# A hybrid decoder layer: eight of its 22 weight units as seven block products, interleaved with the rest

## The chip, the cores and the metric
One core of one Trainium2 chip runs the kernel. The metric is the device time of one execution in microseconds (us); lower is better. The profile is one execution recorded by the hardware profiler. In it PE is TensorE's matmuls, PEld its weight loads, DVE is VectorE, ACT is ScalarE, POOL is GpSimd, and SP is the engine that issues most transfers.

## The reference: what is computed
One decoder layer over 256 tokens `x` and 256 memory tokens `mem`, both 2048 wide, in fp32. `proj = x @ w_in` yields fifteen pieces of 1024 columns: q, k, v and a gate z for block attention; u, v and z for a spatial gating unit; q and z for attention into memory; and three branch gates of 2048 columns.

```python
y_a = _moba_attention(q_a, k_a, v_a) * silu(z_a)          # 8 heads of 128, causal over the 256 tokens
y_g = _spatial_gating(u_g, v_g, w_s, b_s, ln_v_g, ln_v_b) * silu(z_g)
y_c = _memory_attention(q_c, mem @ w_mem_k, mem @ w_mem_v) * silu(z_c)   # 4 heads of 256
gates = sigmoid(g_logit).reshape(b, s, 3, d)
merged = (gates[:, :, 0] * (y_a @ w_branch_attn)
          + gates[:, :, 1] * (y_g @ w_branch_sgu)
          + gates[:, :, 2] * (y_c @ w_branch_mem))
x = _layer_norm(DN_ALPHA * x + merged @ w_out, ln_g, ln_b)
```

The weights make 22 units of 2,097,152 elements (2048x1024, or half of a 1024x2048 pair): 15 in `w_in`, two for the memory's keys and values, three branch projections, two in `w_out`.

## The kernel before, in words
Nearly all arithmetic on TensorE is a product of a weight unit with 256 token columns. To keep fp32 accuracy at the speed of the float32r type, every operand is split: `split` (L41 to L43) writes a high part `hi`, the value rounded to float32r, on ScalarE, and a low part `lo = v - hi` on VectorE. A product then takes three passes: high by high, high by low, low by high.

Weights come in 176 chunks of 1 MB (8 a unit), in the order in which they are used. `load_chunk` issues the load of a chunk on SP's queue (L71) into one of three `raw` buffers; `split_chunk` splits its two halves (128x1024 each) into rings of four `hi` and four `lo` tiles; `feed` loads three chunks ahead and splits one ahead.

There are two forms of product. Channel-major (`channels_out`, L196, with `channels_mm`, L192): the weights are the stationary operand and the moving one holds the high and low parts of 256 tokens, so each block of 128x128 weights takes a matmul of 512 columns (L193) and one of 256 (L194); the result has channels on the partitions, and `joined` (L206 to L209) adds its two halves. Token-major (`tokens_out`, L163, and the output projection, L553): the tokens are stationary and the moving operand is 512 weight columns, so three matmuls of 512 columns serve a block of 128 inputs, 128 tokens and 512 channels. `vg`, `va`, `mv` and the output projection are token-major; the other 17 units, with all gates and branch projections, are channel-major.

The stages follow one another: `vg`, `u`, `zg` with the spatial mixing; `gated_branch(1)`; `va`, `za`, `q` and `k` with block attention; `gated_branch(0)`; `mv`, `mk`, `zc`, `qc` with memory attention; `gated_branch(2)`; output projection, residual and layer norm. Attention works on split parts too (`mm3`, L186: three matmuls for each product). `pending` and `tick` spread the stages of a head over the tiles of the next projection. `gated_branch` (L335 to L360) computes gate tiles with a sigmoid, then branch tiles, multiplies them and sums the three branches in `macc`; the last one splits the sum into `mhl`, the operand of the output projection. The order of each engine's instructions is not the program's: a planner, `TileContext(nc, schedule_with_timeline_sim=True)`, lays them out by the times it expects, and assigns each tile a free buffer of its tag.

## Time and profile before

| what | value |
|---|---|
| median of 3 runs | 1031.0 us (1030.88 to 1031.11) |
| span of the profiled execution | 1029.1 us |
| median minus span | 1.9 us |
| TensorE busy | 1016.3 us, 99% |
| VectorE busy | 628.8 us, 61% |
| ScalarE busy | 519.9 us, 51% |
| moved | 198.06 MB, 192 GB/s over the span |

The profile gives the span, from the first to the last instruction; the profiled execution's own time is not recorded apart from it, so the 1.9 us that the median lies above the span stand for what lies around it. Matmuls are pipelined and the profile models their ends, so the duration of one matmul is longer than the distance to the next; prices are best read from a whole stretch divided by its count. The granted clock was 1.00 wherever TensorE had work.

### The profile page before, as it was taken

What the parts mean: (1) busy time and instruction counts of PE and PEld (TensorE: products, weight loads), DVE (VectorE), ACT (ScalarE), POOL (GpSimd) and SP (SyncE); (2) the same over time, 40 slices, a digit from 0 to 9 for tenths busy, and PEclk for the clock granted to TensorE, in tenths of its full rate; (3) what the DMA queues carried; (4) which work ended last, traced back from release to release, by engine and by line L of the source; (5) the groups of instructions that cost most, each with busy time, mean ns of one, the idle gap of its engine ahead of it and who ended that gap; (6) DMA issues with size and microseconds to landing.
All of it is one profiled execution on the core that took longest, in us unless ns stands there. A gap on an engine that the chain in (4) does not pass through costs nothing.

```text
span 1029.1 us, 14329 instructions
## 1 busy us (share of the span) xinstructions
PE 1016.3 (99%) x5672; PEld 883.2 (86%) x5672; DVE 628.8 (61%) x888; ACT 519.9 (51%) x781; POOL 2.7 (0%) x10
## 2 busy tenths in 40 slices
PE   9999999999999999999999999999999999999995
PEld 7888888888888888888888888888888888888885
DVE  5584665556545456776866664556566576666756
ACT  6465554444445445557644543446455655555430
POOL 0000000000000000000000000000000000000000
PEclk9999999999999999999999999999999999999998
DMA  9855455545555544444655555545553555557722
GB/s 344 326 179 204 164 179 190 203 171 199 197 178 199 187 181 168 165 166 167 246 183 187 204 180 189 203 171 198 179 184 130 204 210 199 179 189 278 256 80 82
DMA packets 31300, 198.06 MB, mean 192 GB/s; under 512 B 3457, under 2 KB 4225, under 8 KB 8705
## 3 DMA queue, kind: packets, MB, share of 16 engines
q1 hardware_dynamic: 30672, 192.95, 52.3%
q10 hardware_dynamic: 560, 4.19, 1.1%
q8 instruction: 44, 0.72, 0.3%
q14 instruction: 24, 0.19, 0.0%
HBM read 195.04 MB, written 2.10 MB: 192 GB/s over the span
## 4 chain that ended last, share of the span: by engine, by line
PE 98%; DVE 1%; DMA 0%; DVEq 0%; ACT 0%; issue 0%; SPq 0%
PE g L193 17%; PE g L194 9%; PE b L193 9%; PE b L194 4%; PE za L193 3%; PE zc L193 3%; PE mk L193 3%; PE qc L193 3%; PE q L193 3%; PE k L193 3%; PE u L193 3%; PE zg L193 3%; PE o L558 3%; PE o L556 3%; PE o L557 3%; PE vg L178 2%
## 5 line engine op out<-in xcount | busy, mean ns | idle before, releaser
L43 DVE TENSOR_TENSOR lo<-raw,hi 128x1024 fp32r<-128x1024 f32 (+1 forms) x350 | 426.3, 1218 | 345.6 <-ACT hi L42 343.9
L42 ACT ACTIVATE hi<-raw 128x1024 fp32r<-128x1024 f32 (+1 forms) x350 | 369.5, 1056 | 432.3 <-PE g L193 116.7
L193 PE MATMUL g<-xhl,hi 128*128 128x512 f32 x768 | 270.3, 395 | 0.0
L194 PE MATMUL g<-xhl,lo 128*128 128x256 f32 x768 | 214.9, 280 | 0.0
L193 PEld LDWEIGHTS g<-xhl,hi 128*128 128x128 f32 x768 | 144.0, 188 | 33.4
L194 PEld LDWEIGHTS g<-xhl,lo 128*128 128x128 f32 x768 | 144.9, 189 | 0.2
L193 PE MATMUL b<-yhl,hi 128*128 128x512 f32 x384 | 135.6, 395 | 0.0
L194 PE MATMUL b<-yhl,lo 128*128 128x256 f32 x384 | 107.2, 280 | 0.0
L193 PEld LDWEIGHTS b<-yhl,hi 128*128 128x128 f32 x384 | 71.9, 188 | 16.4
L194 PEld LDWEIGHTS b<-yhl,lo 128*128 128x128 f32 x384 | 72.4, 189 | 0.2
L556 PE MATMUL o<-hi,mhl 128*128 128x512 f32 (+1 forms) x128 | 46.4, 363 | 0.0
L557 PE MATMUL o<-lo,mhl 128*128 128x512 f32 (+1 forms) x128 | 46.4, 362 | 0.0
L558 PE MATMUL o<-hi,mhl 128*128 128x512 f32 (+1 forms) x128 | 46.4, 362 | 0.0
L193 PE MATMUL q<-xhl,hi 128*128 128x512 f32 x128 | 45.8, 398 | 0.0
L193 PE MATMUL k<-xhl,hi 128*128 128x512 f32 x128 | 45.7, 396 | 0.0
L193 PE MATMUL qc<-xhl,hi 128*128 128x512 f32 x128 | 45.7, 399 | 0.0
L193 PE MATMUL zg<-xhl,hi 128*128 128x512 f32 x128 | 45.3, 397 | 0.0
L193 PE MATMUL zc<-xhl,hi 128*128 128x512 f32 x128 | 45.3, 399 | 0.0
L193 PE MATMUL za<-xhl,hi 128*128 128x512 f32 x128 | 45.3, 399 | 0.0
L193 PE MATMUL mk<-memhl,hi 128*128 128x512 f32 x128 | 45.3, 399 | 0.0
L193 PE MATMUL u<-xhl,hi 128*128 128x512 f32 x128 | 44.8, 396 | 0.0
L194 PE MATMUL q<-xhl,lo 128*128 128x256 f32 x128 | 36.4, 284 | 0.0
(217 smaller groups left out, 1572.8 us busy)
## 6 DMA issues: line engine op xcount, KB each, us to landing
raw<-in_w_gate_dram SPq DMA_DIRECT2D x48, 1024.0 KB, 4.8
raw<-in_w_br_dram SPq DMA_DIRECT2D x24, 1024.0 KB, 4.8
raw<-in_w_qk_dram SPq DMA_DIRECT2D x16, 1024.0 KB, 4.8
raw<-in_w_o_dram SPq DMA_DIRECT2D x16, 1024.0 KB, 4.7
raw<-in_w_ug_dram SPq DMA_DIRECT2D x8, 1024.0 KB, 5.1
raw<-in_w_zg_dram SPq DMA_DIRECT2D x8, 1024.0 KB, 4.8
raw<-in_w_va_dram SPq DMA_DIRECT2D x8, 1024.0 KB, 4.8
raw<-in_w_za_dram SPq DMA_DIRECT2D x8, 1024.0 KB, 4.8
```

The source lines that it names most:

```text
L42: nc.scalar.activation(hi, v, AF.Copy)
L43: nc.vector.tensor_tensor(lo, v, hi.bitcast(F32), op=ALU.subtract)
L178: nc.tensor.matmul(ps[t][n], xh, hi[:, n * 512:(n + 1) * 512], start=(k == 0), stop=False)
L193: nc.tensor.matmul(ps, hi, xhl[:, k, :], start=first, stop=False)
L194: nc.tensor.matmul(ps[:, S:2 * S], lo, xhl[:, k, 0:S], start=False, stop=last)
L556: nc.tensor.matmul(ps[:, 0:n], mh, hi, start=first, stop=False)
L557: nc.tensor.matmul(ps[:, 0:n], mh, lo, start=False, stop=False)
L558: nc.tensor.matmul(ps[:, 0:n], ml, hi, start=False, stop=last)
```

## The change
Eight units (the six gate units, `va` and `vg`) leave the chunk stream. Each is a product of a 256x2048 matrix with a 2048x1024 one, cut into two by two blocks. Seven block products in the Winograd order (`PRODUCTS`) replace the eight of the plain form. The sums of blocks of x are formed once (`sums`), split and stored in DRAM, and read again for each unit (`xsf`). The differences of weight blocks are formed on VectorE in place (`sub` in `s_prep`) for three of the seven products and once more for a fourth, and every product's weight operand is split, 2048 columns at a time. The products accumulate in four PSUM banks, with copies (`keep`) of intermediate sums on ScalarE and final additions (`result`) on VectorE. A unit is 14 steps: half of each of the seven products, 12 matmuls of 512 columns.

The memory's values and keys come first, on their own. After that `classic`, the stream of all other units, runs together with `s_stream`: a loop takes a step of `classic` (half a chunk: 2.8 us or so of matmuls) and, in proportion, steps of the product stream, so that 112 product steps go with the `classic` steps 3 to 146. The order of the branches is now memory, block attention, spatial gating. The branch projections become token-major (`gated_branch`), as their gates are; the gates' logits are stored in DRAM by the product stream and loaded again, `mk`, `mv`, `va`, the z and u tiles and the running sum of branches likewise, and the merged result is transposed on TensorE (`merged`). Attention multiplies unsplit fp32 operands, one matmul for each product. The raw chunk buffers go from three to two, the rings of `hi` and `lo` from four to three; all transfers are issued on SP's queue.

```diff
+    def new_acc(name):
+        return psum.tile([P, 512], F32, tag="acc", name=name, bufs=3)
+    def new_sps(name):
+        return psum.tile([P, 512], F32, tag="sps", name=name, bufs=3)
+    def new_aux(name, shape):
+        return psum.tile(list(shape), F32, tag="aux", name=name, bufs=2)
...
+    late, pending = [], []
+    def step(run):
+        old = late[:]
+        del late[:]
+        run()
+        for fn in old:
+            fn()
...
+        t = wts.tile([P, 2, 1024], F32, tag="raw", name=f"raw{i}", bufs=2)
+        raw[i] = t
...
+    def c_half(ahead=2):
+        while len(ready) < ahead + 1 and ptr["half"] < 2 * len(chunks):
+            prep_half()
+        return ready.pop(0)
...
-    def gated_branch(b):
-        sg = {}
-        for m in range(8):
-            for n in gates_before(m):
-                ps = channels_out(xhl, f"g{b}_{n}")
-                g = work.tile([P, S], F32, tag="gate", name=f"sg{b}_{n}", bufs=4)
-                joined(g, ps)
-                nc.scalar.activation(g, g, AF.Sigmoid)
-                sg[n] = g
-                tick()
-            halves = next_chunk()
-            for i in range(2):
-                n = 2 * m + i
-                hi, lo = halves[i]
-                ps = new_acc(f"b{b}_{n}")
-                for k in range(8):
-                    channels_mm(ps, yhl[b], k, hi[:, k * P:(k + 1) * P], lo[:, k * P:(k + 1) * P], k == 0, k == 7)
-                br = work.tile([P, S], F32, tag="t256", name=f"br{b}_{n}", bufs=4)
-                joined(br, ps)
-                if order[b] == 0:
-                    nc.vector.tensor_tensor(macc[:, n], br, sg[n], op=ALU.mult)
-                else:
-                    nc.vector.tensor_tensor(br, br, sg[n], op=ALU.mult)
-                    nc.vector.tensor_tensor(macc[:, n], macc[:, n], br, op=ALU.add)
-                if order[b] == 2:
-                    split(mhl[0][:, n, 0:S], mhl[0][:, n, S:2 * S], macc[:, n])
...
+                s1, s2, s3, s4 = (F[g][:, i] for i in range(4))
+                nc.vector.tensor_tensor(s1, a21, a22, op=ALU.add)
+                nc.vector.tensor_tensor(s2, s1, a11, op=ALU.subtract)
+                nc.vector.tensor_tensor(s3, a11, a21, op=ALU.subtract)
+                nc.vector.tensor_tensor(s4, a12, s2, op=ALU.subtract)
...
+                t = wts.tile([P, 4, 2 * P], F32R, tag="xsf", name=f"xw{g}{i}", bufs=3)
+                split(t[:, :, 0:P], t[:, :, P:2 * P], F[g][:, i])
+                late.append(lambda: nc.sync.dma_start(xf_d[i + 1, g], t.bitcast(F32)))
...
+    UNITS = 8
+    PRODUCTS = ("M1", "M5", "M6", "M3", "M7", "M4", "M2")
+    FORM = {"M5": 1, "M6": 2, "M3": 4, "M7": 3}
+    rt, shl, xsf, sp = {}, {}, {}, {}
...
+    def s_load(u, blk, h):
+        if u >= UNITS:
             return
...
+        tag, bufs = ("rA", 2) if blk == 0 else ("rB", 4)
+        t = wts.tile([P, 2048], F32, tag=tag, name=f"b{blk}_{u}_{h}", bufs=bufs)
+        nc.sync.dma_start(t, w_st[u, blk, h])
+        rt[u, blk, h] = t
...
+    def s_prep(s):
+        u, r = divmod(s, 14)
+        if u >= UNITS:
+            return
+        p, h = divmod(r, 2)
+        p = PRODUCTS[p]
+        if p in FORM:
+            t = wts.tile([P, 4, 2 * P], F32R, tag="xsf", name=f"xf{s}", bufs=3)
+            nc.sync.dma_start(t.bitcast(F32), xf_d[FORM[p], h])
+            xsf[s] = t
+        b = lambda blk: rt[u, blk, h]
+        sub = lambda o, x, y: nc.vector.tensor_tensor(o, x, y, op=ALU.subtract)
+        src = {"M1": B11, "M5": B11, "M6": B11, "M4": B11, "M3": B22, "M7": B12, "M2": B21}[p]
+        if p == "M5":
+            sub(b(B11), b(B12), b(B11))
+        elif p == "M6":
+            sub(b(B11), b(B22), b(B11))
+        elif p == "M4":
+            sub(b(B11), b(B21), b(B11))
+        hi = wts.tile([P, 2048], F32R, tag="shl", name=f"sh{s}", bufs=4)
+        lo = wts.tile([P, 2048], F32R, tag="shl", name=f"sl{s}", bufs=4)
+        split(hi, lo, b(src))
+        shl[s] = (hi, lo)
+        if p == "M3":
+            sub(b(B12), b(B22), b(B12))
+            s_load(u, B21, h)
+        elif p == "M7":
+            s_load(u + 1, B12, h)
+        elif p == "M4":
+            s_load(u + 1, B11, h)
+        elif p == "M2":
+            s_load(u + 1, B22, h)
...
+        def keep(name, ps):
+            kept[name] = snap(name)
+            nc.scalar.activation(kept[name], ps, AF.Copy)
+        def result(u, t, n, ps, name):
+            r = kept[name]
+            nc.vector.tensor_tensor(r, ps, r, op=ALU.add)
+            finish(u, t, n, r)
+        def evacuate(u, p):
+            if p == "M1":
+                keep(f"k1_{u}", bank["b"])
+            elif p == "M5":
+                keep(f"k5_{u}", bank["d"])
+            elif p == "M6":
+                keep(f"k6_{u}", bank["b"])
+            elif p == "M3":
+                result(u, 0, 1, bank["d"], f"k6_{u}")
+            elif p == "M7":
+                keep(f"k7_{u}", bank["b"])
+                result(u, 1, 1, bank["b"], f"k5_{u}")
+            elif p == "M4":
+                result(u, 1, 0, bank["c"], f"k7_{u}")
+            else:
+                result(u, 0, 0, bank["a"], f"k1_{u}")
+        BANK = {"M1": "b", "M6": "b", "M7": "b", "M5": "d", "M3": "d", "M4": "c", "M2": "a"}
+        for s in range(14 * UNITS):
+            u, r = divmod(s, 14)
+            p, h = divmod(r, 2)
+            p = PRODUCTS[p]
+            if h == 0 and p in ("M1", "M5", "M4", "M2"):
+                bank[BANK[p]] = new_sps(f"s{p}_{u}")
+            ps = bank[BANK[p]]
+            hi, lo = shl.pop(s)
+            for kk in range(4):
+                k = 4 * h + kk
+                if p in FORM:
+                    ah, al = xsf[s][:, kk, 0:P], xsf[s][:, kk, P:2 * P]
+                else:
+                    k += 0 if p == "M1" else 8
+                    t = P if p == "M4" else 0
+                    ah, al = xhl[:, k, t:t + P], xhl[:, k, S + t:S + t + P]
+                c = slice(kk * 512, (kk + 1) * 512)
+                first = h == 0 and kk == 0 and p in ("M1", "M5", "M4", "M2")
+                last = h == 1 and kk == 3
+                nc.tensor.matmul(ps, ah, hi[:, c], start=first, stop=False, skip_group_check=True)
+                nc.tensor.matmul(ps, ah, lo[:, c], start=False, stop=False, skip_group_check=True)
+                nc.tensor.matmul(ps, al, hi[:, c], start=False, stop=last, skip_group_check=True)
+            xsf.pop(s, None)
+            s_prep(s + 2)
+            if h == 1:
+                late.append(lambda u=u, p=p: evacuate(u, p))
+            yield
...
+    for _ in run(mem_values()):
+        pass
+    for i, _ in enumerate(run(mem_keys())):
+        if i >= 1 and x_work:
+            x_work.pop(0)()
+    while x_work:
+        x_work.pop(0)()
+        step(lambda: None)
+    for blk in (B11, B12, B22):
+        for h in range(2):
+            s_load(0, blk, h)
+    s_prep(0)
+    s_prep(1)
...
+            ps = new_aux(f"ms{h}", (P, 2, S))
+            for t in range(2):
+                for kk in range(2):
+                    nc.tensor.matmul(ps[:, t], q[kk][:, t * P:(t + 1) * P], st["k"][:, kk],
+                                     start=(t == 0 and kk == 0), stop=(t == 1 and kk == 1), skip_group_check=True)
...
+            nc.tensor.matmul(ps[:, P:384], q[:, P:S], k, start=False, stop=True, skip_group_check=True)
...
+            nc.tensor.matmul(ps, st["v"][:, 0], st["pt"][:, 0:S], start=True, stop=False, skip_group_check=True)
+            nc.tensor.matmul(ps[:, P:S], st["v"][:, 1], st["pt"][:, S:384], start=False, stop=True,
+                             skip_group_check=True)
...
+    def gated_branch(b, order):
+        for n in range(4):
+            ps = [new_acc(f"b{b}_{n}{t}") for t in range(2)]
+            g, prev = {}, {}
+            for t in range(2):
+                g[t] = w2(f"sg{b}{t}{n}")
+                nc.sync.dma_start(g[t], gl_d[b, t, n])
+                nc.scalar.activation(g[t], g[t], AF.Sigmoid)
+            for half in range(4):
+                hi, lo = c_half()
+                for kk in range(2):
+                    k = 2 * half + kk
+                    c = slice(kk * 512, (kk + 1) * 512)
+                    for t in range(2):
+                        yh, yl = (yhl[b][:, k, o + t * P:o + (t + 1) * P] for o in (0, S))
+                        nc.tensor.matmul(ps[t], yh, hi[:, c], start=(k == 0), stop=False)
+                        nc.tensor.matmul(ps[t], yh, lo[:, c], start=False, stop=False)
+                        nc.tensor.matmul(ps[t], yl, hi[:, c], start=False, stop=(k == 7))
+                if half == 3:
+                    late.append(lambda n=n, ps=ps, g=g: gated(b, order, n, ps, g))
+                yield
+    def gated(b, order, n, ps, g):
+        for t in range(2):
+            if order:
+                prev = w2(f"mp{b}{t}{n}")
+                nc.sync.dma_start(prev, mc_d[order - 1, t, n])
+            nc.vector.tensor_tensor(g[t], ps[t], g[t], op=ALU.mult)
+            if order:
+                nc.vector.tensor_tensor(g[t], g[t], prev, op=ALU.add)
+            if order < 2:
+                store(mc_d[order, t, n], g[t])
+            else:
+                pending.append([lambda t=t: merged(n, t, g[t])])
         tick()
...
+    def merged(n, t, m):
+        if t == 0:
+            mhl.append(wts.tile([P, 4, 2 * S], F32R, tag="shl", name=f"mhl{n}", bufs=4))
+        ps = new_aux(f"mT{n}{t}", (P, 4, P))
+        for i in range(4):
+            nc.tensor.transpose(ps[:, i], m[:, i * P:(i + 1) * P], ident)
+        split(mhl[n][:, :, t * P:(t + 1) * P], mhl[n][:, :, S + t * P:S + (t + 1) * P], ps)
...
+    def s_finish(u, t, n, r):
+        if u in GATES:
+            b, half = GATES[u]
+            store(gl_d[b, t, 2 * half + n], r)
+        elif u == 2:
+            store(va_d[t, n], r)
+        else:
+            if vg[0] is None:
+                vg[0] = big.tile([P, 2, W], F32, tag="vg", name="vg")
+            nc.scalar.activation(vg[0][:, t, n * 512:(n + 1) * 512], r, AF.Copy)
+            if (t, n) == (0, 0):
+                pending.append(sgu_norm())
+    GATES = {0: (2, 0), 1: (2, 1), 3: (0, 0), 4: (0, 1), 6: (1, 0), 7: (1, 1)}
+    def classic():
+        yield from gate_tiles("zc", AF.Silu, szc_d)
+        new_y(2)
+        yield from mem_attention()
+        yield from drain()
+        yield from gated_branch(2, 0)
+        yield from gate_tiles("za", AF.Silu, sza_d)
+        new_y(0)
+        yield from block_attention()
+        yield from drain()
+        yield from gated_branch(0, 1)
+        yield from gate_tiles("ug", AF.Gelu_apprx_tanh, gu_d)
+        new_y(1)
+        yield from gating()
+        yield from drain()
+        yield from gated_branch(1, 2)
+    def drain():
+        yield None
+        while pending:
+            tick()
+            yield None
+    C_STEPS, S_STEPS = 160, 14 * UNITS
+    LEAD, TAIL = 2, 14
+    cs, ss = classic(), s_stream(s_finish)
+    done_c = done_s = 0
+    for _ in run(cs):
+        done_c += 1
+        while done_s < S_STEPS and done_s * (C_STEPS - LEAD - TAIL) < (done_c - LEAD) * S_STEPS:
+            step(lambda: next(ss))
+            done_s += 1
...
+    def blocks(w):
+        b = w.reshape(2, 2, 4, P, 2, 512).transpose(0, 4, 1, 3, 2, 5).reshape(2, 2, 2, P, D)
+        return np.stack([b[0, 0], b[0, 1], b[1, 1], b[1, 0]])
```

## Rows read from the trace of the kernel before
**Rows 1.** The page: busy time of each engine; the chain that ended last, by engine.
```profile
PE 1016.3 (99%) x5672; PEld 883.2 (86%) x5672; DVE 628.8 (61%) x888; ACT 519.9 (51%) x781; POOL 2.7 (0%) x10
...
PE 98%; DVE 1%; DMA 0%; DVEq 0%; ACT 0%; issue 0%; SPq 0%
```
**Rows 2.** Windows by stage: stretch, length, busy us (instructions) by engine, clock, DMA share, GB/s.
```profile
50.90:96.20 45.30, 45.30 (x262) 39.49 (x261) 31.73 (x43) 25.89 (x38) 0.00 (x0) 1.00 0.53 189
...
143.50:277.00 133.50, 133.50 (x774) 117.73 (x773) 78.24 (x102) 66.47 (x100) 0.00 (x0) 1.00 0.52 187
277.00:320.50 43.50, 43.50 (x194) 35.99 (x193) 20.77 (x21) 18.11 (x19) 0.00 (x0) 1.00 0.54 191
320.50:365.80 45.30, 45.30 (x258) 39.24 (x257) 24.30 (x27) 23.48 (x34) 0.00 (x0) 1.00 0.53 189
...
929.30:994.50 65.20, 65.20 (x289) 54.01 (x288) 41.24 (x49) 30.18 (x31) 0.00 (x0) 1.00 0.64 232
994.50:1018.00 23.50, 23.44 (x194) 23.17 (x192) 12.95 (x32) 2.55 (x3) 0.00 (x0) 1.00 0.13 45
```
**Rows 3.** Waits over the span: us in total, times, longest us.
```profile
DVE lo L43 <- ACT hi L42: 343.9, 288, 3.2
ACT hi L42 <- PE g L193: 116.7, 81, 2.6
```
**Rows 4.** Timeline of ScalarE and VectorE in the token-major unit `va`.
```profile
290.98 1.06 ACT L42 ACTIVATE hi<-raw 128x1024 fp32r<-128x1024 f32 x1 [1.66 <-PE va L182]
...
292.07 1.23 DVE L43 TENSOR_TENSOR lo<-raw,hi 128x1024 fp32r<-128x1024 f32 x1 [1.49 <-ACT hi L42]
```
**Rows 5.** Timeline of TensorE around fp32 matmuls (two records each) and transposes.
```profile
71.34 0.61 PE L307 MATMUL mix<-bsw,vg 128*128 128x128 f32 x4
71.70 0.36 PE L194 MATMUL u<-xhl,lo 128*128 128x256 f32 x1
71.91 0.40 PE L193 MATMUL u<-xhl,hi 128*128 128x512 f32 x1
...
764.05 0.27 PE L513 MATMUL mpt<-ident,mp 128*128 128x128 f32 x1
764.08 0.36 PE L194 MATMUL qc<-xhl,lo 128*128 128x256 f32 x1
764.28 0.49 PE L513 MATMUL mpt<-ident,mp 128*128 128x128 f32 x3
764.52 0.47 PE L193 MATMUL qc<-xhl,hi 128*128 128x512 f32 x1
```
**Rows 6.** Groups of VectorE by form: count, busy us, mean ns, idle before.
```profile
L43 DVE TENSOR_TENSOR lo<-raw,hi 128x1024 fp32r<-128x1024 f32 x346 | 423.5, 1225 | 342.8 <-ACT hi L42 341.2
L209 DVE TENSOR_TENSOR sg<-g,evlo 128x256 f32<-128x256 f32 x48 | 20.0, 418 | 0.0
L43 DVE TENSOR_TENSOR lo<-raw,hi 128x512 fp32r<-128x512 f32 x4 | 2.8, 692 | 2.8 <-ACT hi L42 2.7
```
**Rows 7.** Timeline of ScalarE and VectorE in the first gated branch.
```profile
181.17 0.36 ACT L208 ACTIVATE evlo<-b 128x256 f32<-128x256 f32 x1
181.43 0.41 ACT L342 ACTIVATE sg<-sg 128x256 f32<-128x256 f32 x1
...
181.30 1.23 DVE L43 TENSOR_TENSOR lo<-raw,hi 128x1024 fp32r<-128x1024 f32 x1 [1.20 <-ACT hi L42]
182.44 0.41 DVE L209 TENSOR_TENSOR br<-b,evlo 128x256 f32<-128x256 f32 x1
184.02 1.23 DVE L43 TENSOR_TENSOR lo<-raw,hi 128x1024 fp32r<-128x1024 f32 x1 [0.71 <-ACT hi L42]
185.16 0.42 DVE L209 TENSOR_TENSOR br<-b,evlo 128x256 f32<-128x256 f32 x1
```
**Rows 8.** Groups of ScalarE by form.
```profile
L42 ACT ACTIVATE hi<-raw 128x1024 fp32r<-128x1024 f32 x346 | 367.0, 1061 | 429.4 <-PE g L193 116.7 <-issue 82.9 <-PE o L558 33.9
L42 ACT ACTIVATE hi<-raw 128x512 fp32r<-128x512 f32 x4 | 2.5, 631 | 2.8 <-DMA raw<-in_w_vg_dram 2.8
```
**Rows 9.** Transfers: GB/s in 40 slices; issues with count, KB each, us to landing.
```profile
GB/s 344 326 179 204 164 179 190 203 171 199 197 178 199 187 181 168 165 166 167 246 183 187 204 180 189 203 171 198 179 184 130 204 210 199 179 189 278 256 80 82
...
raw<-in_w_gate_dram SPq DMA_DIRECT2D x48, 1024.0 KB, 4.8
raw<-in_w_vg_dram SPq DMA_DIRECT2D x4, 1024.0 KB, 8.0
```
**Rows 10.** Waits of SP's queue.
```profile
SPq L71 <- DVE br L209: 126.5, 23, 10.4
```

More of the change, by code (lines that the diff above doesn't have):

```diff
@@ L196, in channels_out @@
-    def channels_out(xhl, name):
-        halves = next_chunk()
-        ps = new_acc(name)
-        for k in range(KT):
-            hi, lo = halves[k // 8]
-            c = (k % 8) * P
-            channels_mm(ps, xhl, k, hi[:, c:c + P], lo[:, c:c + P], k == 0, k == KT - 1)
-        return ps
-    def joined(out_ap, ps):
-        lo = work.tile([P, S], F32, tag="evlo", name="evlo", bufs=2)
+    chunks, held_at = [], {}
+    raw, ready, act_raw = {}, [], {}
+    ptr = {"load": 0, "half": 0}
+    hold = {}
@@ L381, in decoder_layer, with mem_attention, fin @@
+    def mem_attention():
+        for h in range(MH):
+            q = [w1(f"qc{h}{kk}") for kk in range(2)]
+            fetch, stages = mem_head(h, q)
+            fetch()
+            for kk in range(2):
+                def fin(ps, kk=kk, q=q):
+                    joined(q[kk], ps, f"qc{h}{kk}")
+                yield from channel_tile(x_k, f"qc{h}_{kk}", fin)
+            late.append(lambda stages=stages: pending.append(stages))
     SC = float(P) ** -0.5
[L383 removed]
```

711 lines of the change are left out of this document (342 added, 369 removed).

## The prediction
> **What bounds the kernel now.** I read four views in this order. First the page's busy times and its chain of waits: TensorE works 99% of the span, and 98% of the chain that ended last is TensorE's; VectorE is busy 628.8 us, ScalarE 519.9 us [rows 1]. Second, the windows by stage: in all thirteen stages between 50.9 and 994.5 us TensorE's busy time equals the length of the stage, at a granted clock of 1.00, while VectorE is busy for 48 to 70% of it [rows 2]. So the reader is to see a kernel that ends when its matmuls end. Third, the waits: VectorE's low parts stand waiting for ScalarE's high parts for 343.9 us, and those wait for TensorE to give back a buffer [rows 3]; they are waits of engines with time to spare. In a token-major stretch both wait once in each period of 2.72 us [rows 4]. Fourth, groups by form, for the prices.
>
> TensorE's price comes from the windows. Token-major, `va` takes 43.5 us for its 192 matmuls of 512 columns: 0.2266 us each. Channel-major, the gates and branches take 133.5 us for three units; taking 0.7 us of mixing off leaves 44.3 a unit; `za` took 45.3. The last 23.5 us hold 194 matmuls of 256 columns: 0.12 us each [rows 2].
>
> **The change, TensorE's side.** A unit of 2048x1024 weights needs 192 matmuls of 512 columns token-major. Seven products of half size in all three dimensions need 7 x 24 = 168, so 168 x 0.2266 = 38.1 us.
> - Six gate units go from 44.3 to 38.1: -37.2 us.
> - `va` and `vg` go from 43.5 to 38.1: -10.8 us.
> - Three branch units go from channel-major to token-major, 44.3 to 43.5: -2.4 us.
> - Attention goes from three matmuls on parts to one in fp32. Two fp32 matmuls of 128 columns and one part matmul of 256 take 71.34 to 71.91 [rows 5], so one of 128 columns costs (0.57 - 0.12)/2 = 0.225 us; one of 256, which the trace lacks, I take as twice that less one fixed part, 0.44 (bounds 0.225 and 0.45). A memory head goes from 24 x 0.12 = 2.9 to 8 x 0.44 = 3.5 us, four heads: +2.6. A block head loses six matmuls of 0.12 and gains two of 0.44: +0.16, eight heads: +1.3.
> - The merged result is now token-major and has to be transposed: 32 transposes. Four of them and a 256-column matmul take 764.05 to 764.52 [rows 5]: 0.088 each, +2.8 us.
>
> Sum: -50.4 + 6.7 = -43.7. From the span of 1029.1 us that leaves 985.4, if TensorE is fed as well as now.
>
> **VectorE's side.** This is where the change pays. A 1024-wide low part lasts 1.225 us, a 512-wide one 0.69, a 256-wide one 0.42 [rows 6]; behind one another the 1024-wide take 1.14 (181.30 to 182.44, 184.02 to 185.16) [rows 7]. The slope from 512 to 1024 is 1.055 ns a column, so a 2048-wide operation, which the trace lacks, should take 2.2 us (1.14 + 1024 x 1.04 ns); it is bounded by 1.14, and by 2.45, two of the single ones. I take 2.2.
> A step of the product stream is one half of one product: a low part (2.2), in 64 of 112 steps a block difference (2.2), and 32 additions of results over the 112 steps (0.65 each). That makes 2.2 + 1.26 + 0.19 = 3.65 us, against 12 x 0.2266 = 2.72 us on TensorE. A half chunk of the other units costs VectorE 1.14 plus half a join of 0.42, and TensorE 2.8.
> The loop gives 112 product steps to C steps 3 to 146, of which about 10 are empty drain steps; so the two streams run together over 136 half chunks, up to the middle of `zg`. VectorE there: 136 x 1.14 = 155; 112 x 2.2 = 246; 64 x 2.2 = 141; results 21; 52 joins 22; gating of two branches 16; both attentions 36; gating unit 16; together about 655 us. TensorE there: six and a half channel units 294; two branches 87; products 304.5; attention, transposes and mixing 30; together 716 us. So VectorE would be busy 91% of a stretch where today it is busy 59% (78.24 of 133.50) [rows 2]. TensorE still bounds it, with 61 us between them.
> ScalarE: 224 high parts of 1.06, 112 of about 1.95, 32 copies of 0.6 and what it had make some 600 us of the span [rows 8], of which about 450 fall in the mixed stretch (136 x 1.06, 112 x 1.95, the rest copies and activations); TensorE's 716 us cover them. Should the cover go, it is the same wait as the first rival's.
>
> **What I add for stalls.** The two drains give some eight product steps with no other matmuls; there VectorE's 3.65 stands against 2.72: 7 us if nothing is pulled ahead, 0 if the planner moves branch matmuls in (it does move: in [rows 7] the sigmoid of a gate at 181.43 stands behind the copy of the next tile). After the last branch, product and sum on VectorE, four transposes, a split (0.69 + 0.69 + 0.35 + 0.6 + 0.69) stand before the last quarter of the output projection: 3 us, or 0 if the first three quarters cover it. The start has two raw buffers for three: 0 to 2 us. Bounds 0 and 12; I take 12, since these phases have the least cover, so 997.4 of span.
>
> **Transfers.** The chunks of the product units are as many bytes as before. New are the sums of x, read 64 times 0.5 MB, and the stores and loads of gates, `va`, `mk`, `mv` and running sums, about 25 MB. In the mixed stretch 64 + 68 + 34 + 25 = 191 MB move in 716 us: 267 GB/s, where slices of now reach 344 and an ordinary load lands in 4.8 us, one at the start's load in 8.0 [rows 9]. A half chunk is wanted three C steps (some 15 us) after its buffer is given back, so TensorE's work hides 8 us. All of it now goes by SP's queue: behind a store that waits for VectorE's result stand the loads of weights of both streams, and for them ScalarE's high parts. SP waits today for VectorE up to 10.4 us [rows 10]. I cost it at nothing (below: nothing to gain; above: the second rival).
>
> **Rivals.**
> 1. *VectorE's queue becomes the bound.* After a block difference VectorE has to wait for ScalarE's high part (1.95 us) before the low part; if nothing else is ready behind it, it stands idle. For it: the low parts wait for ScalarE 288 times now [rows 3], 1.49 us each in [rows 4]. Against it: there the high part itself waits for TensorE (1.66 us), and a buffer pair comes back two product steps ahead, 2 x 6.4 us, for a chain of 2.72 + 1.95 + 2.2. Price: all 112 waits unfilled are 218 us, less the 61 to spare: 157, a time of 1144 (985.4 + 157 + 1.9). Slower than now is reached at 61 + 44 = 105 us of idleness in the stretch, 0.94 us a step, just under half of the wait. Half the wait, 109 us, gives 985 + 48 + 2 = 1035. A mild form, 85 to 104 us idle, gives 1011 to 1030.
> The Trainium skill, TensorE: Matmul & The Clock Gate, "Architectural detail: the array is 16× 32×32, not 1× 128×128", says that the vector engine's queue is strictly first in, first out, so that what stands behind a waiting low part waits with it. By that rule alone, with low parts queued right behind their differences, it would be 1144; the trace agrees on the order within a queue (the copies at 182.44 and 185.16 follow the waited-for low parts [rows 7]), but the planner chooses that order, so I give the case a minority.
> 2. *Loads come late.* If stores that wait up to 10.4 us hold SP's queue and a load then needs 8, the 15 us are overrun by 3 us; over some 68 chunks, one in six to one in three late, that is 34 to 68 us: 1021 to 1055.
> 3. *The products save nothing in matmuls of their own pace.* Channel-major units vary from 44.3 to 45.3 [rows 2] with no wait seen; if the products took 2% more the same way, that is 6 us: about 1005, inside my range.
>
> **How the numbers follow.** The runs' median is 1031.0, 1.9 us above the profiled span; 997.4 + 1.9 = 999.3, and I say 999. Its own range is 983 to 1010, with a chance of 0.58 (0.03 of it for rival 3); the floor is 985.4 + 1.9 = 987, less 4 for the uncertain unit prices (44.3 against 45.3). Rival 1's mild form, 1011 to 1030, has 0.16; its hard form, 1033 and up, 0.14; rival 2 has 0.12, of which 0.06 is faster, 0.02 the same and 0.04 slower than now. Faster by over 0.2%: 0.58 + 0.16 + 0.06 = 0.80; slower by over 0.2%: 0.18; within 0.2%, about what a measurement of this kernel can tell from no change: 0.02. To 1034 the cases hold over 0.8, so the range is 982 to 1034.
>
> **What the profile after should show.** If right: TensorE still 97% or more busy of a span near 997; some 38 us of matmuls for each product unit at 0.227 each; VectorE about 850 us busy (1.14 x 224 + 2.2 x 176 + some 200 of smaller ones); 2048-wide operations of 2.2 to 2.3 us; idle TensorE only near the drains and the end of branch 1. If rival 1 holds: TensorE's waits name VectorE's `lo` of the product stream spread over the whole mixed stretch, and VectorE's own idle time names ScalarE. If rival 2 holds: ScalarE's high parts wait for DMA. A granted clock below 1.00 in a stage with work, which no stage now shows [rows 2], would make the prediction wrong as well, as would a 2048-wide operation of 2.45 us, which takes 44 of the 61 us to spare.

## The result and the profile after

The changed kernel takes 1037.8 us (median of 4 runs, 1036.3 to 1040.8) against 1031.05 (1030.88 to 1031.48): a ratio of 1.0069, with a 95% interval of 1.0052 to 1.0085. It is slower by 6.7 us where 32 us less were forecast, and it lies outside the range of 982 to 1034. The profiled execution took 1036.3 us with a span of 1034.6.

The page, its busy times and its chain by engine:

```profile
PE 987.9 (95%) x4888; PEld 827.9 (80%) x4888; DVE 823.0 (80%) x800; ACT 580.4 (56%) x638; POOL 7.8 (1%) x17
...
PE 74%; DMA 11%; DVE 8%; ACT 3%; issue 3%; SPq 0%; DVEq 0%; ACTq 0%
```

TensorE's busy time fell from 1016.3 to 987.9 us [rows 1] and its instructions from 5672 to 4888, but now it is busy for 95% of a longer span, and a fifth of the chain belongs to transfers and VectorE, where all but 2% was TensorE's.

The groups of VectorE by form (busy us, mean ns of one, idle before), which answer to [rows 6]:

```profile
L60 DVE TENSOR_TENSOR lo<-raw,hi 128x1024 fp32r<-128x1024 f32 x214 | 259.1, 1220 | 95.8 <-ACT hi L59 94.7 <-PE q L166 0.3
L60 DVE TENSOR_TENSOR sl<-b,sh 128x2048 fp32r<-128x2048 f32 x112 | 255.9, 2287 | 56.5 <-ACT sh L59 55.8
...
L289 DVE TENSOR_TENSOR b<-b,b 128x2048 f32<-128x2048 f32 x64 | 145.8, 2283 | 6.2 <-DMA b<-in_w_st_dram 6.0
```

The prices held: 2.28 us for a 2048-wide operation, 823 us of VectorE in all. So the loss is one of place. Windows of 25 us (length, busy us of TensorE, its weight loads, VectorE, ScalarE and GpSimd with counts, granted clock, DMA share, GB/s) show where. A window in which TensorE was full stands between them for comparison:

```profile
0.00:25.00 25.00, 21.63 (x88) 16.61 (x88) 16.73 (x24) 16.61 (x24) 1.56 (x9) 1.00 0.90 337
25.00:50.00 25.00, 15.99 (x61) 12.24 (x62) 17.08 (x20) 11.09 (x13) 0.00 (x0) 0.86 1.02 417
50.00:75.00 25.00, 22.77 (x102) 18.02 (x101) 12.01 (x13) 9.38 (x12) 0.00 (x0) 0.96 1.02 409
...
300.00:325.00 25.00, 19.49 (x83) 14.38 (x81) 25.00 (x20) 12.19 (x15) 0.00 (x0) 1.00 0.30 111
...
475.00:500.00 25.00, 25.00 (x129) 21.10 (x128) 23.17 (x16) 13.26 (x12) 0.00 (x0) 1.00 0.53 186
...
650.00:675.00 25.00, 18.95 (x83) 14.57 (x81) 22.72 (x21) 17.94 (x21) 0.00 (x0) 0.97 0.49 194
675.00:700.00 25.00, 20.72 (x68) 15.92 (x69) 21.11 (x28) 16.68 (x21) 0.00 (x0) 0.75 0.45 147
...
750.00:775.00 25.00, 21.79 (x100) 17.99 (x99) 25.00 (x22) 11.98 (x13) 0.00 (x0) 0.93 0.52 172
```

From 75 to 300, 350 to 625 and 775 to 1000 us TensorE is busy all the time, as before. It has holes in two sorts of place. At the **start** DMA is at a share of 1.02 and 417 GB/s, and TensorE idles 3.4 + 9.0 + 2.2 = 14.6 us. The **drains** are the stretches in which `classic` has only the heads' last stages and the branch's matmuls to give, ahead of `za` (about 300 to 325) and ahead of `ug` (650 to 700); they idle 5.5 us and 6.1 + 4.3 us. The end of the second branch (750 to 775) idles another 3.2: there a chunk's load is issued only at 761.76, when VectorE's low part (760.52 + 1.22) has given back its buffer. In all of them VectorE is busy 21 to 25 of 25 us and the transfers are slack. The four longest holes (8.0, 4.1, 3.2 and 3.0 us) are each followed by a stretch in which TensorE is busy with few matmuls, at a granted clock below 1.00: 68 instructions in the 20.7 busy us of 675 to 700. After the shorter ones that is not always so: ahead of `za`, where no hole is longer than 1.4 us, the clock stays at 1.00.

The second drain closer: the timelines of VectorE, ScalarE and TensorE (start, us; the bracket is the idle time before, and what ended it). On VectorE's and ScalarE's lines `b` is a weight block; on TensorE's it is a branch's result, and `sM` a sum of the product stream.

```profile
667.33 0.55 DVE L553 SCALAR_TENSOR_TENSOR p<-s,mask 128x384 f32<-128x384 f32 x1
667.79 0.68 DVE L612 BATCH_NORM_STATS2 vst<-vg 128x6 f32<-128x512 f32 x1
668.39 4.47 DVE L289 TENSOR_TENSOR b<-b,b 128x2048 f32<-128x2048 f32 x2
672.78 2.28 DVE L60 TENSOR_TENSOR sl<-b,sh 128x2048 fp32r<-128x2048 f32 x1
674.99 0.28 DVE L557 TENSOR_REDUCE mx<-p 128x1 f32<-128x128 f32 x1
...
682.59 0.15 DVE L561 RECIPROCAL sm<-sm 128x2 f32<-128x2 f32 x1
```
```profile
665.94 1.91 ACT L59 ACTIVATE sh<-b 128x2048 fp32r<-128x2048 f32 x1 [2.01 <-PE sM L365]
...
676.92 0.19 ACT L559 ACTIVATION_READ_ACCUMULATOR p<-p,mx 128x1 f32 x1
```
```profile
670.43 0.39 PE L688 MATMUL b<-hi,yhl 128*128 128x512 f32 x1
670.66 0.39 PE L689 MATMUL b<-lo,yhl 128*128 128x512 f32 x1
675.12 0.79 PE L365 MATMUL sM<-sl,xf 128*128 128x512 f32 x1 [4.08 <-DVE sl L60]
675.72 0.63 PE L366 MATMUL sM<-sh,xf 128*128 128x512 f32 x1
676.14 0.63 PE L364 MATMUL sM<-sh,xf 128*128 128x512 f32 x1
```

The next matmul in TensorE's queue is one on the low part `sl` of 672.78; the branch's next ones (L690) need a low part of `yhl`, which VectorE writes at 675.18. Its high part was done at 667.85 (665.94 + 1.91); what stands ahead of it on VectorE are two block differences of later steps (668.39, 4.47 us). TensorE stands for 4.08 us. The head fares likewise: its `p` of 667.33 was done at 667.88, its maximum is taken at 674.99; the sums for its reciprocal were read at 677.11 (676.92 + 0.19), the reciprocal runs at 682.59. That is 7.1 and 5.5 us of waiting in VectorE's queue, in a chain that the drain has to wait for. After the hole of 4.08 us the matmuls start 0.42 us apart where 0.23 is the rule, at the granted clock's lower level, 1.2 of 2.4 GHz; the five-us window that starts at 675.00 has 0.50.

The start, by transfers: SP's queue in the first 20 us, then issues of the first 70 us (count, KB each, median us from issue to landing), which answer to [rows 9].

```profile
12.60 1.29 SPq L230 DMA_DIRECT2D X<-in_xT_dram  x2
13.94 1.06 SPq L273 DMA_DIRECT2D b<-in_w_st_dram  x2
15.34 5.28 SPq L105 DMA_DIRECT2D raw<-in_w_mv_dram  x3
```
```profile
b<-in_w_st_dram SPq DMA_DIRECT2D x6, 1024.0 KB, 11.5
raw<-in_w_mv_dram SPq DMA_DIRECT2D x4, 1024.0 KB, 10.1
```

While the first unit `mv` waits for its chunks, the planner issues X and the blocks of the first product unit among them; a chunk then lands in 10.1 us, where 8.0 was the start's and 4.8 the ordinary case before [rows 9]. The first unit's 208 TensorE instructions take 64 us, at 0.95 of the clock, where the first unit before took 51. One window of each kernel, the changed one first:

```profile
0.00:64.00 64.00, 51.56 (x208) 39.77 (x208) 41.42 (x51) 34.19 (x43) 1.56 (x9) 0.95 0.97 387
```
```profile
0.00:51.00 51.00, 49.36 (x208) 40.75 (x209) 28.83 (x31) 27.68 (x33) 2.66 (x10) 1.00 0.88 334
```

### The profile page after: what moved, and what is told of

It is laid out like the page before. It is cut to its first block, busy times and chain, and to the rows that moved or that the text cites. A ratio compares the mean times of both kernels' runs of the same rounds, so it can differ in the third digit from the quotient of the medians.

```text
span 1034.6 us, 12910 instructions
## 1 busy us (share of the span) xinstructions
PE 987.9 (95%) x4888; PEld 827.9 (80%) x4888; DVE 823.0 (80%) x800; ACT 580.4 (56%) x638; POOL 7.8 (1%) x17
## 4 chain that ended last, share of the span: by engine, by line
PE 74%; DMA 11%; DVE 8%; ACT 3%; issue 3%; SPq 0%; DVEq 0%; ACTq 0%
PE sM L365 7%; PE sM L364 7%; PE sM L366 7%; DMA raw<-in_w_mv_dram 4%; DVE sl L60 3%; PE mk L165 3%; PE q L165 3%; PE za L165 3%; PE zc L165 3%; PE qc L165 3%; PE k L165 3%; PE zg L165 3%; PE o L782 3%; PE o L781 3%; PE o L780 3%
## 5 line engine op out<-in xcount | busy, mean ns | idle before, releaser
L59 ACT ACTIVATE hi<-raw 128x1024 fp32r<-128x1024 f32 (+1 forms) x218 | 227.8, 1050 | 213.4 <-DMA raw<-in_w_o_dram 22.2
L60 DVE TENSOR_TENSOR lo<-raw,hi 128x1024 fp32r<-128x1024 f32 (+1 forms) x218 | 261.8, 1210 | 98.7 <-ACT hi L59 97.7
L60 DVE TENSOR_TENSOR sl<-b,sh 128x2048 fp32r<-128x2048 f32 x112 | 255.9, 2287 | 56.5 <-ACT sh L59 55.8
L59 ACT ACTIVATE sh<-b 128x2048 fp32r<-128x2048 f32 x112 | 214.5, 1915 | 123.2 <-PE sM L365 101.8
L289 DVE TENSOR_TENSOR b<-b,b 128x2048 f32<-128x2048 f32 x64 | 145.8, 2283 | 6.2 <-DMA b<-in_w_st_dram 6.0
L365 PE MATMUL sM<-sl,xf 128*128 128x512 f32 x256 | 103.6, 405 | 5.7 <-DVE sl L60 5.7
L364 PE MATMUL sM<-sh,xf 128*128 128x512 f32 x256 | 102.8, 402 | 1.1 <-ACT sh L59 1.1
L366 PE MATMUL sM<-sh,xf 128*128 128x512 f32 x256 | 102.6, 401 | 0.0
L364 PE MATMUL sM<-sh,xhl 128*128 128x512 f32 x192 | 76.0, 396 | 0.0
L366 PE MATMUL sM<-sh,xhl 128*128 128x512 f32 x192 | 75.1, 391 | 0.0
L690 PE MATMUL b<-hi,yhl 128*128 128x512 f32 x192 | 74.0, 391 | 1.0 <-DVE yhl L60 1.0
L688 PE MATMUL b<-hi,yhl 128*128 128x512 f32 x192 | 71.7, 391 | 1.6 <-ACT hi L59 1.6
L364 PEld LDWEIGHTS sM<-sh,xf 128*128 128x128 f32 x256 | 49.3, 193 | 12.5 <-ACT sh L59 1.7
L366 PEld LDWEIGHTS sM<-sh,xf 128*128 128x128 f32 x256 | 49.5, 193 | 10.6
```

The source lines that it names most:

```text
L59: nc.scalar.activation(hi, v, AF.Copy)
L60: nc.vector.tensor_tensor(lo, v, hi.bitcast(F32), op=ALU.subtract)
L289: sub = lambda o, x, y: nc.vector.tensor_tensor(o, x, y, op=ALU.subtract)
L364: nc.tensor.matmul(ps, ah, hi[:, c], start=first, stop=False, skip_group_check=True)
L365: nc.tensor.matmul(ps, ah, lo[:, c], start=False, stop=False, skip_group_check=True)
L366: nc.tensor.matmul(ps, al, hi[:, c], start=False, stop=last, skip_group_check=True)
```

## The experiments

Theory A, formed on this trace: TensorE's sum was right, and what is lost is lost at the start, to transfers, and in the drains, to VectorE's product work without other matmuls as cover. Rival B: VectorE holds back the whole stretch, so less VectorE work helps everywhere. Rival C: the drains are the latency of the heads' chains, whatever VectorE does besides. The kernels without block differences (e4, e5, e11) leave work out, so what they compute is not the layer; they show only what that work costs. Times against the kernel before (1030.9 to 1031.0 beside each run):

| run | what | us | ratio (95%) |
|---|---|---|---|
| e1_start | loads of the start held back | 1034.7 | 1.0038 (1.0028 to 1.0048) |
| e2_order | drains filled by reordering | 1008.5 | 0.9782 (0.9763 to 0.9800) |
| e3_both | e1 and e2 | 1004.8 | 0.9748 (0.9733 to 0.9762) |
| e4_nosub | no block differences | 1008.7 | 0.9784 (0.9768 to 0.9801) |
| e5_order_nosub | e2 and e4 | 1005.5 | 0.9753 (0.9736 to 0.9769) |
| e6_order_pool | e2, differences on GpSimd | 1119.7 | 1.0859 (1.0833 to 1.0886) |
| e7_late | e2, product stream starts later | 999.96 | 0.9702 (0.9687 to 0.9716) |
| e8_late_pool | e7, differences on GpSimd | 1114.7 | 1.0814 (1.0782 to 1.0847) |
| e9_pause | no product steps emitted in drains | 1035.7 | 1.0048 (1.0033 to 1.0063) |
| e10_late_only | late start, order as changed | 1022.8 | 0.9921 (0.9906 to 0.9935) |
| e11_late_nosub | e7 and e4 | 991.4 | 0.9625 (0.9604 to 0.9645) |

**The drains: e2_order and e4_nosub.** The first changes the order alone, so that each drain has a unit of `classic` matmuls instead (the chunk list, not shown, follows the same order):

```diff
 def classic():
     ...
     yield from mem_attention()
+    yield from gate_tiles("za", AF.Silu, sza_d)
     yield from drain()
     yield from gated_branch(2, 0)
-    yield from gate_tiles("za", AF.Silu, sza_d)
     ...
     yield from block_attention()
+    yield from gate_tiles("ug", AF.Gelu_apprx_tanh, gu_d)
     yield from drain()
     yield from gated_branch(0, 1)
-    yield from gate_tiles("ug", AF.Gelu_apprx_tanh, gu_d)
```

> Only the order of the classic stream is changed: the z tiles of block attention come between memory attention and its branch, the u tiles of the gating unit between block attention and its branch, so that the heads' last stages run under matmuls and no step of the stream is empty. Theory A: most of the 25 us of the drains goes, 1013 to 1023 us. Rival B: VectorE has the same work in the same stretch, so 1030 or more.

Measured: 1008.5, 29.3 us less than the changed kernel and more than theory A gave it (1013 to 1023). The start keeps its hole (TensorE is busy 14.7 us from 25 to 50), and from 125 to 775 us TensorE is busy in every microsecond. Two of its windows, same columns as above, where the changed kernel has its drains:

```profile
300.00:325.00 25.00, 25.00 (x131) 21.39 (x130) 21.34 (x22) 18.52 (x26) 0.00 (x0) 1.00 0.59 205
...
675.00:700.00 25.00, 25.00 (x129) 21.18 (x128) 22.10 (x19) 22.11 (x26) 0.00 (x0) 1.00 0.61 226
```

VectorE has all its differences there and is busy 568 of the 650 us, 87%: with other matmuls as cover that leaves TensorE full. The second leaves the order and takes 146 us off VectorE:

```diff
-        sub = lambda o, x, y: nc.vector.tensor_tensor(o, x, y, op=ALU.subtract)
+        sub = lambda o, x, y: None
```

> The changed kernel without the 64 block differences on VectorE (the products are taken of undiffered blocks, so the result is not the reference's); it takes 146 us of work from VectorE and nothing else. Theory A: the drains' stalls go, the start's stay, 1010 to 1018 us. Rival C (the drains' stalls are the latency of the heads' chains or late loads, not VectorE's load): 1030 or more. Rival B: the mixed stretch shrinks as well outside the drains, below 1008.

Measured: 1008.7, 29.0 us less, between theory A's range (1010 to 1018) and rival B's (below 1008). The two windows in which the changed kernel has its second drain:

```profile
650.00:675.00 25.00, 23.13 (x100) 18.44 (x100) 21.49 (x22) 24.87 (x26) 0.00 (x0) 1.00 0.68 248
675.00:700.00 25.00, 25.00 (x112) 20.70 (x111) 21.44 (x24) 16.38 (x17) 0.00 (x0) 1.00 0.88 306
```

The heads' work is the same here, and `za` and `ug` still come behind the branches; yet TensorE is busy 48.1 of 50 us at full clock, where it was busy 39.7 at 0.97 and 0.75, and from 75 to 650 us it has no hole. So it is not the heads' chain by itself that makes the drain long, but VectorE's 2.28 us operations in it. The edit takes away two things at once, the time of the differences and the wait of a high part for its difference (2.35 us before the `sh` of 672.90 in the changed kernel, which the timeline's cut leaves out); no run parts them. Both edits give 29 us; the next run tells whether it is the same 29.

**e5_order_nosub**, both edits together.

> The reordered stream without the 64 block differences on VectorE (so the result is not the reference's). Each edit alone took 29 us off the changed kernel (1008.5 and 1008.7). Theory A: VectorE limits TensorE only in the drains, so both edits remove the same stalls and do not add: 1002 to 1008 us. Rival B (VectorE bounds the mixed stretch as a whole): they add, 975 to 990 us.

Measured: 1005.5, only 3.0 below e2, about as much as the runs of one kernel scatter (1006.3 to 1011.0 for e2). The two edits heal the same loss; with the drains covered, 146 us less of VectorE's work are worth some 3 us. Rival B falls as the main cause.

**The start: e1_start and e3_both.** X is held behind two chunks of `mv`, the six block loads behind chunks of `mk`:

```diff
-            nc.sync.dma_start(t[:, h], chunks[i][:, h])
+            loaded[i] = nc.sync.dma_start(t[:, h], chunks[i][:, h])
...
-                    x_loads[kp - 5]()
+                    with tc.issue_after(loaded[kp].ins):
+                        x_loads[kp - 5]()
...
-    for blk in (B11, B12, B22):
+    for blk, c in ((B11, 12), (B12, 8), (B22, 14)):
         for h in range(2):
-            s_load(0, blk, h)
+            with tc.issue_after(loaded[c + h].ins):
+                s_load(0, blk, h)
```

> Only the order on SP's queue at the start is changed: the two loads of x stand behind the memory-value chunks 5 and 6, the six first block loads behind memory-key chunks 8, 9 and 12 to 15. Theory A (the loss lies in four places: some 20 us at the start, where early loads of the product stream take bandwidth from the chunks of the memory values, 25 us in the two drains, 5 us around the change from branch to gating unit; elsewhere TensorE is full): the start's loss goes, 1018 to 1023 us. Rival B (VectorE bounds the whole mixed stretch, and what TensorE loses in one place it would lose in another): 1033 or more.

> Both edits of the two kernels before. Theory A: the gains add, 995 to 1006 us, clearly below the kernel before the change (1031). Rival B: 1028 or more.

Measured: 1034.7, 3.1 us less than the changed kernel, and with the reordering 1004.8, 3.7 less than without. So e1 alone missed theory A's 1018 to 1023 and fell into rival B's range (1033 or more), though not for rival B's reason, as its windows show:

```profile
25.00:50.00 25.00, 24.71 (x109) 20.09 (x109) 22.23 (x26) 15.29 (x18) 0.00 (x0) 1.00 0.91 328
50.00:75.00 25.00, 19.91 (x100) 16.43 (x99) 12.97 (x14) 11.03 (x14) 0.00 (x0) 0.93 1.02 415
75.00:100.00 25.00, 22.82 (x121) 19.50 (x120) 10.19 (x11) 9.54 (x12) 0.00 (x0) 0.93 1.03 411
```

The hole of 25 to 50 us is gone and stands at 50 to 100 instead, again at 411 to 415 GB/s. The loss is one of bytes that two streams want in the same 100 us, not of the order alone. Nor is it VectorE's work on the sums of X: from 25 to 50 us VectorE is busy 22.2 us here, and TensorE 24.7. What a third `raw` buffer, which the kernel before had, would give back was not tried.

**e7_late** takes the reordering and moves the bytes: the product stream starts ten `classic` steps late, its first six blocks are loaded one by one during them. X is held behind two chunks of `mv` as in e1 (that part and the reordering are not shown again).

```diff
-    for blk in (B11, B12, B22):
-        for h in range(2):
-            s_load(0, blk, h)
-    s_prep(0)
-    s_prep(1)
...
-    LEAD, TAIL = 2, 14
+    LEAD, TAIL = 10, 14
+    first = {1: (B11, 0), 2: (B11, 1), 3: (B12, 0), 4: (B12, 1), 6: (B22, 0), 7: (B22, 1)}
     ...
         done_c += 1
+        if done_c in first:
+            with tc.issue_after(loaded[max(loaded)].ins):
+                s_load(0, *first[done_c])
+        if done_c in (LEAD - 2, LEAD - 1):
+            s_prep(done_c - LEAD + 2)
```

> The reordered stream with the product stream started later: 10 steps of the classic stream go ahead instead of 2, the first six block loads (6 MB) are issued one by one behind the chunks of the first classic steps, the loads of x behind memory-value chunks 5 and 6. In the first 100 us the changed kernel moves 33 to 36 MB, up to 417 GB/s from 25 to 75 us. Theory A1 (the start is short of bandwidth, so that a new order of the same bytes only shifts the stall, as in the first kernel of this study, and fewer early bytes remove it): most of the start's 15 to 20 us go, 990 to 998 us. Rival (the start is lost to something else, VectorE's and ScalarE's work on the sums of x or the two raw buffers): 1003 to 1008 us.

Measured: 999.96 us, 8.5 below e2, 37.8 below the changed kernel, and 3.0% below the kernel before (2.8 to 3.1%). It lies between the two ranges, 990 to 998 if the start's bytes were all, 1003 to 1008 if they were not.

**e10_late_only**, the late start (with X held back) without the reordering.

> The changed kernel in its own order with the late start alone: the product stream leads by 10 steps and not 2, its first six block loads are issued one by one behind chunks of the first classic units, and the X loads behind two mv chunks. Theory A (start and drains are two separate losses): about what the late start gave on top of the reordering, 8.5 us less 0 to 3, so 1027 to 1032 us, still no faster than before by more than 0.4%. Rival (the start is the larger loss and the reordering only met it by chance): 1020 us or less.

Measured: 1022.8, 15.0 us less than the changed kernel: between what theory A and its rival gave, so both numbers missed. Its first 75 us idle 4.3 us at full clock, where the changed kernel idles 14.6 and loses clock; that is the larger part of the 15. Alone the edits give 29.3 and 15.0, together 37.8: they overlap by 6.5 us, and the late start is worth 8.5 to 15.0, depending on what follows (more on this at e11).

**e9_pause**, against rival C: the order as changed, but the counter that paces the product stream stands still in a drain.

```diff
+    draining = [False]
     def drain():
+        draining[0] = True
         ...
+        draining[0] = False
...
-        done_c += 1
+        done_c += not draining[0]
```

> The changed kernel in its own order; only, while a drain runs (the stretches ahead of za and ahead of ug), the counter that sets the pace of the product stream stands still, so no product step runs there and VectorE has the heads' rows and branches to itself. The steps are made up later beside classic matmuls. Theory A (the product steps in the drains hold up the heads, because VectorE is busy all the time there and no classic matmul covers it): most of the 29 us that the reordering gave comes back, 1010 to 1020 us; TensorE is idle in the drains only for the heads' own chain. Rival C (the chain of the heads and branches from VectorE to ScalarE and back is long by itself, whoever else is on VectorE): 1030 us or more, and the drains show the same idle time with VectorE no longer full.

Measured: 1035.7, which looks like rival C. But the edit didn't do what it was made for. Between 650 and 700 us the trace still has 98 product matmuls (113 in the changed kernel) and, as there, six block differences (busy us, count, in the row of line 289):

```profile
650.00:700.00 50.00, 13.57 (x6) 0.83 0.51 182
```

The planner fills the drain with product steps that the program emits elsewhere. So this run says nothing on rival C; e4_nosub does, and speaks against it. A drain free of product work was not tried.

**e6_order_pool and e8_late_pool** move the differences to GpSimd, to take them off VectorE and keep the result.

```diff
-        sub = lambda o, x, y: nc.vector.tensor_tensor(o, x, y, op=ALU.subtract)
+        sub = lambda o, x, y: nc.gpsimd.tensor_tensor(o, x, y, op=ALU.subtract)
```

> The reordered stream with the 64 block differences on GpSimd in place of VectorE. VectorE's 146 us go to an idle engine, at a price that no run has shown. Theory A: little is to be had, 1001 to 1010 us, if GpSimd needs less than 8 us for one (8 of them in the 90 us of a unit) and its results come in time; slower than 1015 if it needs more or slows VectorE. Rival B: 990 or less.

> The kernel before with the block differences on GpSimd. Theory A: as the kernel before to within 5 us. Rival B: 15 us or more below it.

Measured: 1119.7 and 1114.7, some 111 and 115 us slower than with the differences on VectorE. That is far above theory A's 1001 to 1010 for e6 and its 5 us around e7 for e8; the expectation had named a slower VectorE as the way to fail, and that is what happened. Groups of e6_order_pool by form:

```profile
L60 DVE TENSOR_TENSOR lo<-raw,hi 128x1024 fp32r<-128x1024 f32 x214 | 387.9, 1820 | 89.8 <-ACT hi L59 89.2
L289 POOL TENSOR_TENSOR b<-b,b 128x2048 f32<-128x2048 f32 x64 | 351.4, 5501 | 551.6 <-DVE sl L60 373.9 <-DMA b<-in_w_st_dram 129.9 <-DMA va<-k 28.8
```

A difference takes 5.5 us there, 2.4 times VectorE's (4.57 us at the shortest, so waits are in it), and VectorE, with 146 us of work less, is busy 925 us. One case in its timelines, GpSimd and VectorE:

```profile
484.05 5.13 POOL L289 TENSOR_TENSOR b<-b,b 128x2048 f32<-128x2048 f32 x1 [17.87 <-DMA b<-in_w_st_dram]
```
```profile
484.61 5.65 DVE L60 TENSOR_TENSOR lo<-raw,hi 128x1024 fp32r<-128x1024 f32 x1
```

The low part, 1.22 us by itself, begins within GpSimd's operation and ends 1.08 us after it (490.26 against 489.18): all but 0.14 us of its work lies behind GpSimd's. The Trainium skill, SBUF — State Buffer, "SBUF: two separate sides", says that the two engines share a pair of ports as an exclusive lock for a whole instruction, and that a VectorE operation with two SBUF inputs needs it too beside a GpSimd operation that reads SBUF. This trace agrees.

**e11_late_nosub**, e7 without the differences.

> The best version so far (reordered, late start) without the 64 block differences on VectorE: its products use the first operand alone, so 146 us of VectorE's work are left out and the result isn't the reference's. Theory A (with the drains empty VectorE no longer sets the time; what is left over TensorE's sum is spread start, transfers and the end): 993 to 1000 us. Rival B (VectorE still costs some 10 us in the mixed stretch): 990 us or less.

Measured: 991.4, between the two ranges. Its busy times and two windows:

```profile
PE 974.0 (98%) x4888; PEld 822.4 (83%) x4888; DVE 690.8 (70%) x736; ACT 595.5 (60%) x651; POOL 9.1 (1%) x17
...
75.00:950.00 875.00, 875.00 (x4391) 740.25 (x4390) 615.26 (x624) 548.12 (x591) 7.57 (x8) 1.00 0.75 275
0.00:75.00 75.00, 70.21 (x322) 56.29 (x323) 50.48 (x61) 41.34 (x54) 1.55 (x9) 1.00 0.91 333
```

With this load on VectorE TensorE is busy every microsecond from 75 to 950; 4.8 us are missing at the start, where the kernel before missed 1.6 in its first 51. The span of 990.0 less the 3.2 between them is 986.8, against the sum of 985.4 that was forecast for a TensorE that is fed as well as before. So of the 12.7 us that e7 lies above 987.3 (the sum and the 1.9 around it), 8.6 are VectorE's differences and 4.1 the rest. Rival B is right to this extent.

Against e5, which has the early start and no differences, the late start is worth 14.1 us, much as in e10 (15.0). In e7 it gives back only 8.5, because there the differences cost 8.6 and not 3: the late start packs the 112 product steps beside 136 steps of `classic` (`C_STEPS - LEAD - TAIL`) instead of 144. Two windows of e7, in which VectorE is full and e11 has no hole:

```profile
675.00:700.00 25.00, 23.78 (x105) 19.08 (x104) 25.00 (x21) 15.92 (x18) 0.95 (x1) 1.00 0.32 104
...
775.00:800.00 25.00, 23.57 (x126) 19.58 (x125) 25.00 (x28) 15.60 (x16) 3.55 (x2) 1.00 0.58 205
```

From 675 to 850 us TensorE idles 5.2 us in e7. That the closer packing is the cause is argued from this; no run changes it alone.

## Why the prediction was wrong, point by point

- **TensorE's sum, 985.4: right.** A stretch of pure product matmuls (23 between 300.5 and 305.7) has them 0.227 us apart; e11's TensorE is busy 974.0 us, where 1016.3 less the forecast 43.7 is 972.6, and its span gives 986.8. Rival 3 (products of a slower pace) falls.
- **VectorE's prices: right.** 2.28 us against 2.2 for the wide operations, 823 us against some 850 in all. From 75 to 800 us it is busy 618 of 725, 85% where 91% was forecast. As an average over the stretch the reckoning held, and e2's full TensorE from 125 to 775 us bears it out; e11 shows that with the product steps packed closer the differences still cost 8.6 us.
- **"What I add for stalls", 12 us: the step that failed.** For the drains it took the excess of a product step (3.65 against 2.72), eight times: 7 us. The edits that cover or unload them give back 29. There were more steps, too: 113 product matmuls, over nine steps, run between 650 and 700 us alone. Left out were that the heads' short operations stand in the same queue behind 2.28 us operations, so that the drain itself lasts longer; that differences of later steps are put there, ahead of what is wanted at once; and the lower clock behind a hole. "0 if the planner moves branch matmuls in" had the planner's freedom right, but it moved VectorE's work in as well. The bound of 12 rested on each product step by itself, and the lower clock was put at nothing.
- **"Transfers … I cost it at nothing": failed at the start alone.** The mixed stretch moves its bytes as forecast (262 GB/s from 75 to 800, against 267; counted in the page's MB, with a block or chunk of 1024 KB as 1.05 MB, the forecast's bytes make some 275) and TensorE is full through most of it. But the mean hid the first 75 us, where the change adds X, the sums of its blocks and the first weight blocks to a stage that already moved 344 GB/s [rows 9]. It was put at "0 to 2 us", for buffers; the first unit alone ends 13 us later, and moving the bytes gives back 8.5 to 15.0.
- **Rival 1** (VectorE's queue bounds): the time lies where its hard form was put (1033 and up, 0.14), but it has the right engine and the wrong place: low parts wait for ScalarE for some 150 us in all (94.7 + 55.8 in the groups above), hidden by matmuls; the time went where none were. Its sign, TensorE's waits for the stream's low parts spread over the whole stretch, did not come: they are 8.1 us in seven waits, 4.1 of them in the second drain. Spread over the whole stretch it is refuted by e5, at the pace of the changed kernel. The rule of order within a queue that was cited there is what the drain shows: the maximum at 674.99 stands behind three wide operations. (What the prediction calls copies at 182.44 and 185.16 are VectorE's additions of `joined`.) **Rival 2** (loads late) has the right signature at the start (high parts of `mv` wait for transfers) and in the mixed stretch only at the hole of 3.2 us between 750 and 775, where VectorE gave the buffer back late.
- **What the profile should have shown.** Idle time near the drains came in place, but longer; the end of branch 1, put at 3 us, has none (TensorE is full from 775 to 1000), while the start, put at next to nothing, and the end of the second branch (750 to 775), not named, have some. A granted clock below 1.00 in a stage with work was named as a sign that the forecast is wrong; it stands at 0.75 in the second drain.

The account, by experiments in order: 1037.8, less 29.3 for covered drains, less 8.5 for the later start, less 8.6 for the differences, is 991.4; 4.1 us above the sum are not assigned by a run; the windows put some 3 of them at the start. The split depends on the order of the edits: by e2, e5 and e11 it is 29.3, then 3.0 for the differences and 14.1 for the late start. The lower clock is part of these terms, and no run takes it away alone. An estimate from two pages of the profile: the same 4888 matmuls are busy 987.9 us in the changed kernel, at a mean granted clock of 0.982, and 974.0 in e11, at 0.995. So of the 44.6 us between their spans (1034.6 and 990.0) some 14 are slower matmuls and some 31 idle time, of which the prediction's term for stalls counted only the second kind. That e7 takes 999.96 and the forecast was 999.0 is no merit of the forecast: its 12 us of stalls stood for other things.

## What to carry to other kernels

A saving on the bounding engine that is paid for on another one is safe only where that engine has cover, so reckon it stage by stage: find each stretch in which the bounding engine's other work runs out (a drain, the start), and sum all that is queued there on the paying engine, short operations of other chains among it, instead of the excess of one step. The remedy is to move independent work of the bounding engine into such a stretch; here a swap of two units was worth 29 us, as much as leaving out 146 us of VectorE's work. Transfers likewise: a mean of 267 GB/s over a stretch says nothing on a start that already moves 344.

## What the runs showed of the hardware that had not been expected

- Differences on GpSimd slow VectorE's operations with two SBUF inputs: the low part of 1.22 us took 1.82 on average beside them, the 2.29 us one 2.94, and the single one shown, 5.65 us long, ended only 1.08 us after GpSimd's.
- A hole of 4.08 us on TensorE was followed by matmuls 0.42 instead of 0.23 us apart: the granted clock at 0.50, so that this stall cost more than its length.
- This core's transfers held 417 GB/s over 25 us with a DMA share of 1.02. The Trainium skill, DMA: Bandwidth & Descriptors, "Where 436 GB/s comes from", puts loads from HBM at about 358 GB/s for a core; the measurement is higher, with one core at work, and there a 1 MB load took 10 us and more to land.
